# A third chunk made by seven block products in the first net of a two-layer hybrid model, with memory and parameters waiting in the space of the turned memory

## The chip, the cores and the metric

The kernel runs on one core of one Trainium2 chip. The metric is the device time of one execution in microseconds. Engines are named as the profile names them: PE (TensorE, matmul), PEld (its weight loads), DVE (VectorE), ACT (ScalarE), POOL (GpSimd), SP (SyncE, which here only issues transfers).

## What is computed

Two layers. Each runs a gated feed-forward net, a mixer (short convolution, gated linear recurrence, moving averages), cross attention to a memory of 256 rows, and a second net, each followed by a residual with layer norm:

```python
def swiglu(x, w_gate, w_up, w_down):
    return (jax.nn.silu(x @ w_gate) * (x @ w_up)) @ w_down
...
for l in range(DEPTH):
    h = layer_norm(ALPHA * h + 0.5 * swiglu(h, ffn1_gate[l], ffn1_up[l], ffn1_down[l]), ln_g[l, 0], ln_b[l, 0])
    ...
    h = layer_norm(ALPHA * h + cross_attn(h, mem, ca_q[l], ca_k[l], ca_v[l], ca_o[l]), ln_g[l, 2], ln_b[l, 2])
    h = layer_norm(ALPHA * h + 0.5 * swiglu(h, ffn2_gate[l], ffn2_up[l], ffn2_down[l]), ln_g[l, 3], ln_b[l, 3])
```

There are 256 tokens (two blocks of 128), the model's width is 1024, the width inside a net 2816. All is float32.

## The kernel before, in words

**Splitting.** Every float32 factor is split into a high part, rounded to the PE's float32 format by an ACT copy, and a low part, the rest, by a DVE subtraction (`split`, L60 to L62). A product is three matmuls: high by high, high by low, low by high (`mm_rows`, L129). So each weight tile that a transfer brings (`raw`, 128 partitions by 1024 numbers, 512 KB) costs one ACT copy (`whi`, L61) and one DVE subtraction (`wlo`, L62) before PE can use it. There are six raw tiles, eight high and eight low ones; each waits for its last reader before it is filled again.

**A net** (`ffn`, L400) goes through the inner width in chunks of 512: c = 0 to 4, and a last one, 5, of 256. For a chunk, `hidden` (L538) makes gate and up of both token blocks: 8 weight tiles, 96 matmuls. The turned activations then meet the rows of `down`: after chunk c come `both(c - 2, 1)` and `both(c - 1, 0)` (L696), 24 matmuls and two weight tiles each (after chunk 1 only the second of them, and for chunk 5 other ends).

`by_seven` (L568) makes the same chunk from the 2x2 block product (halves of the depth by token blocks; gate and up are the two columns) with seven block products in place of eight: 84 matmuls. For it, sums of blocks of x are made once (`blocks_of_x`, L552: four `quarters` on DVE at L556, four sums at L564, four splits). Of the weights, four blocks of two tiles are loaded: w00 (gate, upper half), w01 (up, upper), w11 (up, lower) and w10 (gate, lower). PE multiplies by w00, w00 + w01, that + w11, w01 + w11, w11, w10 and the last sum + w10, in this order in PE's program (L624 to L638). The sums are made in place by DVE (L597, eight tiles), and all seven are split (14 tiles). Results are put together by DVE (`put`, L619, seven times) and go through the activation in `left` (L641).

w00 is loaded into `spare0` and `spare1`, w01 into the tiles of the layer norm's scale and shift (`lng`, `lnb`), w11 into two raw tiles, w10 into `spare2` and a raw tile (L588 to L591). In the first net the quarters lie in `lng` and `lnb` too (L685).

Which chunks are made by seven is said at L679: 2 and 4 in three of the four nets, only 4 in the first one (`early` is given there).

**The first net's side work.** The small parameters are read into `spare2` and turned by PE (`small_parameters`, L221). The memory is read by 32 transfers on POOL's queue into `spare0` and `spare1` and later turned by DVE and split into `mT` (`load_memory`, L183). Both are begun behind chunk 1's loads (L729). The memory is turned inside chunk 2 (`aside`, L704), the parameters after it (L731). `keys` (L755), the stage after the first net, is the first reader of `mT`.

**Order.** Each engine's instructions are put in a fixed order when the program is built, by a scheduler that lets loads and splits move ahead as far as their tiles are free; on the chip each engine then takes them in that order, and waits at the first one that isn't ready. `tc.issue_after(ins)` adds an order to `ins` for those instructions of its block that run on the same engine as `ins`, and no wait across engines.

Of the kernel before, what the change touches and what calls it, by code (L numbers as in the profile page):

```python
# [17 lines left out]
P = 128  # L18
# [11 lines left out]
LEVELS = (1, 2, 4, 8, 16, 32, 64)  # L30
WINDOWS = (2, 4, 8, 16)
PAD = 16


class Weights:
# [11 lines left out]
def model(ctx: ExitStack, tc: tile.TileContext, t: dict, out: bass.AP):  # L47
# [112 lines left out]
    )  # L160

    xT = cst.tile([P, NK, 2, SEQ], F32R, name="xT")
    mT = cst.tile([P, NK, 2, SEQ], F32R, name="mT")
    xTh, xTl = xT[:, :, 0, :], xT[:, :, 1, :]
    mTh, mTl = mT[:, :, 0, :], mT[:, :, 1, :]
    kTh = cst.tile([P, NK, SEQ], F32R, name="kTh")
    kTl = cst.tile([P, NK, SEQ], F32R, name="kTl")

# [13 lines left out]

    def load_memory(mp, behind):  # L183
        m = [
            mp.tile([P, DM], F32, tag=f"spare{n}", name="m", bufs=1).rearrange("p (k b j) -> p k b j", k=4, j=32)
            for n in range(2)
        ]
        with tc.issue_after(behind.ins):
            for n in range(2):
                for a in range(4):  # L190
                    for k in range(4):
                        c = (4 * n + k) * P + a * 32
                        nc.gpsimd.dma_start(
                            m[n][a * 32 : a * 32 + 32, k],
                            t["mem"][0, :, c : c + 32].rearrange("(b i) j -> i b j", i=32),
                        )

        def later():
            for n in range(2):
                for k in range(0, 4, 2):  # L200
                    turned = mp.tile([P, 2, SEQ], F32, tag="up", name="turned")
                    nc.vector.transpose(
                        turned.rearrange("p k t -> p (k t)"), m[n][:, k : k + 2].rearrange("p k b j -> p (k b j)")
                    )
                    d = slice(4 * n + k, 4 * n + k + 2)
                    split(mTh[:, d, :], mTl[:, d, :], turned)

        return later

# [9 lines left out]
    psc = prm[:, 28:32].rearrange("p (l j) -> p l j", l=DEPTH)  # L219

    def small_parameters(op):  # L221
        spare = op.tile([P, DM], F32, tag="spare2", name="rows", bufs=1)
        rows = spare[:, 0:P]
        nc.gpsimd.memset(rows, 0.0)
        nc.gpsimd.dma_start(rows[0:12, :], t["conv_w"].rearrange("l k (j p) -> (l k j) p", p=P))
        nc.gpsimd.dma_start(rows[12:20, :], t["rec_lb"].rearrange("l (h p) -> (l h) p", p=P))
        nc.gpsimd.dma_start(rows[20:28, :], t["rec_norm_g"].rearrange("l (h p) -> (l h) p", p=P))
        nc.gpsimd.dma_start(rows[28:32, :], t["pool_scale"].rearrange("l (j p) -> (l j) p", p=P))
        nc.gpsimd.memset(wpool, 0.0)
        for g in range(2):  # L230
# [24 lines left out]

        cnt = op.tile([P, 2, PAD], F32, name="cnt", bufs=1)
        wcol = op.tile([P, 2], F32, name="wcol", bufs=1)
        for g, w in enumerate(WINDOWS):
            nc.gpsimd.memset(wcol[(g % 2) * 64 : (g % 2) * 64 + 64, g // 2 : g // 2 + 1], float(w))
        nc.gpsimd.iota(  # L260
            cnt, pattern=[[0, 2], [1, PAD]], base=1, channel_multiplier=0,
            allow_small_or_imprecise_dtypes=True,
        )

        def later():
            pt = acc((P, P))
            nc.tensor.transpose(pt, rows, idn)
            nc.vector.tensor_copy(prm, pt[:, 0:32])
            for j in range(2):
                nc.vector.tensor_scalar_min(cnt[:, j, :], cnt[:, j, :], wcol[:, j : j + 1])  # L270
            nc.vector.reciprocal(invc, cnt)

            lb = [prm[:, 12:16], prm[:, 16:20]]
            mx = op.tile([P, HEADS], F32, name="mx", bufs=1)
            nc.vector.tensor_tensor(mx, lb[0], lb[1], op=ALU.max)
            e = op.tile([P, DEPTH, HEADS], F32, name="e", bufs=1)
            s = op.tile([P, HEADS], F32, name="s", bufs=1)
            for l in range(DEPTH):
                nc.vector.tensor_tensor(e[:, l, :], lb[l], mx, op=ALU.subtract)
            nc.scalar.activation(e, e, AF.Exp)  # L280
# [119 lines left out]
    def ffn(l, name, n, pend=None, last=False, early=None):  # L400
        gate, up, down = (t[f"{name}_{x}"][l] for x in ("gate", "up", "down"))
        with tc.tile_pool(name="ffn", bufs=2, reuse_waits="tile") as fp:
# [273 lines left out]
                return w, ah[:, 2 * u : 2 * u + 2, :], al[:, 2 * u : 2 * u + 2, :]  # L676


            sevens = (2, 4) if early is None else (4,)  # L679
            bx = []  # L680

            if early is None:
# [21 lines left out]
            def aside():  # L704

                with tc.issue_after(lows[-1].ins):
                    if bx:
                        rest[1]()
                    else:
                        bx.extend(blocks_of_x())  # L710

            for c, (c0, ncol) in enumerate(chunks):
                if not c:
                    acts.append(first())
                    ys = [[acc((P, 512), "dn") for _ in range(2)] for _ in range(NT)]
                elif c in sevens:
                    left = by_seven(c0, bx)
                else:
                    if c in (1, 2) and early is not None:
                        acts.append(hidden(c0, aside))  # L720
                    else:
                        acts.append(hidden(c0) if ncol == CHUNK else last_hidden(c0))
                if c == 1 and early is None:
                    bx.extend(blocks_of_x())
                if c == max(sevens) + 1:
                    gb = ln_params(l, n)
                if c == 1 and early is not None:

                    with tc.issue_after(loads[-1].ins):  # L729
                        rest = early(fp)  # L730
                if c == 2 and early is not None:  # L731
                    with tc.issue_after(lows[-1].ins):
                        rest[0]()
                if c > 0:
                    if c > 1:
                        both(c - 2, 1)
                    if c in sevens:
                        acts.append(left())
                    if c < len(chunks) - 1:
                        both(c - 1, 0)  # L740
# [24 lines left out]
    def values(l, c, vh, vl, between={}):  # L765
        w = load(t["ca_v"][l], 0, NK, c * CHUNK, CHUNK)
        for i in range(NT):
            o = acc((P, 512))
            for k in range(NK):
                if k % 2 == 0:  # L770
                    between.get(4 * i + k // 2, lambda: None)()
                wh, wl = w.at(k, slice(0, CHUNK))
                mm_rows(o, mTh[:, k, tok(i)], mTl[:, k, tok(i)], wh, wl, k == 0, k == NK - 1)
            d = slice(c * CHUNK, (c + 1) * CHUNK)
            split(halves(vh[:, i, d]), halves(vl[:, i, d]), sums(o))

# [404 lines left out]


    def beginnings(op):
        parameters, made = small_parameters(op)
        return parameters, load_memory(op, made)

    pend = None
    for l in range(DEPTH):
# [32 lines left out]
```

## Time and profile before

| | |
|---|---|
| three runs | 1070.62, 1070.91, 1071.72 us; median 1070.91 |
| span of the profiled execution, first to last instruction | 1068.8 us; its own time is not listed apart, and the median of the runs is 2.1 us above its span |
| PE busy | 1059.3 us, 99% |
| DVE busy | 946.3 us, 89% |
| ACT busy | 642.4 us, 60% |
| POOL busy | 66.4 us, 6% |
| granted PE clock, mean | 0.998 |
| moved by DMA | 231.90 MB, mean 217 GB/s |
| first net on PE | from 7.64 us on; chunk 2 begins at 54.44, chunk 4 at 116.71 |

Busy times are of one execution. A matmul row's mean duration is longer than the pace at which matmuls follow each other, since they are pipelined; the pace is read from stretches of the chain that ended last (length by count). In the same way a DVE operation's duration overlaps a little with the next one's, so costs of DVE work are read from start to start.

### The profile page before, as it was taken

The page shows a single profiled execution, that of the slowest core. Times are in us where ns is not written, and L with a number is a line of the kernel's source. Part 1 is how long each engine was busy: PE and PEld are TensorE (multiplying, and loading weights), DVE is VectorE, ACT ScalarE, POOL GpSimd, SP SyncE. Part 2 cuts the span into 40 slices and gives each one's busy share as a digit, 9 for nine tenths or more (in the row PEclk, how much of TensorE's full clock was granted, in tenths as well). Part 3 has the DMA queues.
Part 4 walks back from the last instruction along what each step waited for, and adds up shares of the span by engine and source line. Part 5 has one row for each costly group of instructions (what it writes and reads, how often), then busy time and mean ns, then how long its engine had stood idle before and what let it go on. Part 6 is the DMA issues. An engine that isn't in the chain of part 4 may idle for free.

```text
span 1068.8 us, 16312 instructions
## 1 busy us (share of the span) xinstructions
PE 1059.3 (99%) x5966; PEld 937.7 (88%) x5966; DVE 946.3 (89%) x1318; ACT 642.4 (60%) x916; POOL 66.4 (6%) x114
## 2 busy tenths in 40 slices
PE   9999999999999999999999999999999999999997
PEld 7888888889899888888888888888898998888886
DVE  6977997998988799999799999788989787999996
ACT  7555664666557565656575557566764665656660
POOL 9700001000000000000000000010000000000000
PEclk9999999999999999999999999999999999999999
DMA  9997484755574575848675865856536665759461
GB/s 362 262 307 256 129 288 165 249 176 174 170 278 167 178 252 194 290 167 218 238 272 184 256 254 183 290 179 216 196 126 213 241 227 181 257 156 334 134 223 40
DMA packets 130895, 231.90 MB, mean 217 GB/s; under 512 B 9408, under 2 KB 48608, under 8 KB 130816
## 3 DMA queue, kind: packets, MB, share of 16 engines
q1 hardware_dynamic: 129024, 228.49, 64.8%
q0 software_dynamic: 1216, 1.20, 0.5%
q8 instruction: 47, 0.77, 0.3%
q10 hardware_dynamic: 576, 1.18, 0.3%
q14 instruction: 32, 0.26, 0.1%
HBM read 216.15 MB, written 1.05 MB: 203 GB/s over the span
## 4 chain that ended last, share of the span: by engine, by line
PE 99%; DMA 0%; DVE 0%; issue 0%; DVEq 0%
PE acc L105 65%; PE dn L105 31%; PE acc L172 1%; PE dn L923 1%; PE dn L982 0%; DMA h<-in_x_dram 0%; PE acc L491 0%; PE dn L981 0%; PE dn L971 0%; PE acc L1047 0%; PE dn L888 0%; DVE h L358 0%; DVE h L353 0%; PE dn L472 0%; DVE st L338 0%
## 5 line engine op out<-in xcount | busy, mean ns | idle before, releaser
L61 ACT CAST whi<-raw 128x1024 fp32r<-128x1024 f32 (+1 forms) x438 | 442.9, 1042 | 197.5 <-DVE raw L597 54.9
L62 DVE TENSOR_TENSOR wlo<-raw,whi 128x1024 fp32r<-128x1024 f32 (+1 forms) x438 | 515.7, 1209 | 32.6 <-ACT whi L61 29.0
L105 PE MATMUL acc<-whi,xT 128*128 128x512 f32 x1032 | 312.9, 380 | 0.0
L105 PEld LDWEIGHTS acc<-whi,xT 128*128 128x128 f32 x1032 | 195.1, 189 | 27.5
L105 PE MATMUL acc<-wlo,xT 128*128 128x512 f32 x516 | 195.6, 379 | 0.0
L105 PE MATMUL acc<-xT,whi 128*128 128x512 f32 x576 | 142.3, 383 | 0.2
L105 PE MATMUL dn<-whi,ah 128*128 128x512 f32 x346 | 131.5, 380 | 0.0
L105 PE MATMUL dn<-wlo,ah 128*128 128x512 f32 x346 | 131.2, 379 | 0.0
L105 PE MATMUL dn<-whi,al 128*128 128x512 f32 x346 | 131.2, 379 | 0.0
L105 PEld LDWEIGHTS acc<-xT,whi 128*128 128x128 f32 x576 | 104.0, 190 | 12.5 <-ACT whi L61 0.7
L105 PEld LDWEIGHTS acc<-wlo,xT 128*128 128x128 f32 x516 | 97.5, 189 | 13.8
L105 PE MATMUL dn<-whi,xT 128*128 128x512 f32 x288 | 87.9, 381 | 0.0
L105 PEld LDWEIGHTS acc<-xT,wlo 128*128 128x128 f32 x576 | 75.5, 191 | 3.9
L105 PE MATMUL acc<-xT,wlo 128*128 128x256 f32 x576 | 75.9, 275 | 0.0
L105 PEld LDWEIGHTS dn<-whi,al 128*128 128x128 f32 x346 | 65.4, 189 | 9.2
L105 PEld LDWEIGHTS dn<-wlo,ah 128*128 128x128 f32 x346 | 65.4, 189 | 9.2
L105 PEld LDWEIGHTS dn<-whi,ah 128*128 128x128 f32 x346 | 65.4, 189 | 9.1
L350 POOL TENSOR_TENSOR rs<-rs,nhalf 128x1 f32<-128x1 f32 x16 | 14.9, 930 | 833.6 <-DVE rs L346 598.1
L597 DVE TENSOR_TENSOR raw<-raw 128x1024 f32<-128x1024 f32 x56 | 66.2, 1217 | 0.4
L105 PEld LDWEIGHTS dn<-whi,xT 128*128 128x128 f32 x288 | 54.4, 189 | 7.7 <-DVE xT L62 0.3
L105 PE MATMUL dn<-wlo,xT 128*128 128x512 f32 x144 | 54.6, 379 | 0.0
L332 DVE SCALAR_TENSOR_TENSOR h<-h,dn 128x512 f32<-128x512 f32 x31 | 21.2, 683 | 32.9 <-PE dn L105 32.9
(234 smaller groups left out, 1277.5 us busy)
## 6 DMA issues: line engine op xcount, KB each, us to landing
raw<-in_ffn_up_dram SPq DMA_DIRECT2D x88, 512.0 KB, 5.3
raw<-in_ffn_down_dram SPq DMA_DIRECT2D x88, 512.0 KB, 6.6
raw<-in_ffn_gate_dram SPq DMA_DIRECT2D x84, 512.0 KB, 5.1
raw<-in_w_in_dram SPq DMA_DIRECT2D x48, 512.0 KB, 4.7
dealt<-sg SPq DMA_DIRECT2D x80, 128.0 KB, 4.7
raw<-in_ca_k_dram SPq DMA_DIRECT2D x16, 512.0 KB, 4.9
raw<-in_w_out_dram SPq DMA_DIRECT2D x16, 512.0 KB, 4.5
raw<-in_ca_v_dram SPq DMA_DIRECT2D x16, 512.0 KB, 5.3
```

Of the source, the lines that this page charges most:

```text
L61: nc.scalar.copy(hi, src)
L62: lows.append(nc.vector.tensor_tensor(lo, src, hi.bitcast(F32), op=ALU.subtract))
L105: nc.tensor.matmul(o, w, x, start=start, stop=stop)
L172: nc.tensor.transpose(pt[:, k, :], src[:, (4 * j + k) * P : (4 * j + k + 1) * P], unit)
L332: nc.vector.scalar_tensor_tensor(v, v, ALPHA / scale, sums(y[i][n]), op0=ALU.mult, op1=ALU.add, accum_out=None if junk is None else st[:, ...
L350: nc.gpsimd.tensor_tensor(rs, rs, nhalf[:, 0:1], op=ALU.pow)
L597: nc.vector.tensor_tensor(r[i], r[i], plus[i], op=ALU.add)
L923: nc.tensor.matmul(o[g, hh, :], kc[:, hh, g], x, start=True, stop=True)
```

## The change

The first net, too, makes chunk 2 by seven. For that `spare0` to `spare2` must be free at chunk 2. So the parameters' rows and the memory get the space in which the turned memory will lie: two tiles, `mT0` (first rows, then the first half of the turned memory) and `mT1` (first the memory as it was read, then the second half). A small class, `Halves`, makes the two look like one. The parameters are turned after chunk 3's products are written down (c == 3), the memory after chunk 5's (c == 5), and the call that loads the memory stands at c == 3.

```diff
+class Halves:
+    def __init__(self):
+        self.tiles = [None, None]
+    def __getitem__(self, at):
+        k = at[1]
+        if isinstance(k, slice):
+            n = k.start // 4
+            return self.tiles[n][(at[0], slice(k.start - 4 * n, k.stop - 4 * n), *at[2:])]
+        return self.tiles[k // 4][(at[0], k % 4, *at[2:])]
...
-    mT = cst.tile([P, NK, 2, SEQ], F32R, name="mT")
+    mT = Halves()
+    early_rows, early_memory = (cst.tile([P, 2048], F32, tag=f"mT{n}", name=f"early{n}") for n in range(2))
...
     def load_memory(mp, behind):
         m = [
-            mp.tile([P, DM], F32, tag=f"spare{n}", name="m", bufs=1).rearrange("p (k b j) -> p k b j", k=4, j=32)
-            for n in range(2)
+            early_memory[:, n * DM : (n + 1) * DM].rearrange("p (k b j) -> p k b j", k=4, j=32) for n in range(2)
         ]
...
         def later():
             for n in range(2):
-                for k in range(0, 4, 2):
-                    turned = mp.tile([P, 2, SEQ], F32, tag="up", name="turned")
+                turned = [mp.tile([P, 2, SEQ], F32, tag="up", name="turned") for _ in range(2)]
+                for k in range(2):
                     nc.vector.transpose(
...
+                mT.tiles[n] = cst.tile([P, 4, 2, SEQ], F32R, tag=f"mT{n}", name=f"mT{n}")
+                for k in range(2):
+                    d = slice(4 * n + 2 * k, 4 * n + 2 * k + 2)
+                    split(mT[:, d, 0, :], mT[:, d, 1, :], turned[k])
...
     def small_parameters(op):
-        spare = op.tile([P, DM], F32, tag="spare2", name="rows", bufs=1)
+        spare = early_rows[:, 0:DM]
...
-            sevens = (2, 4) if early is None else (4,)
+            sevens = (2, 4)
...
                 with tc.issue_after(lows[-1].ins):
-                    if bx:
-                        rest[1]()
-                    else:
-                        bx.extend(blocks_of_x())
+                    bx.extend(blocks_of_x())
...
-                    if c in (1, 2) and early is not None:
+                    if c == 1 and early is not None:
                         acts.append(hidden(c0, aside))
...
-                if c == 2 and early is not None:
+                if c == 3 and early is not None:
                     with tc.issue_after(lows[-1].ins):
                         rest[0]()
+                    turn_memory = load_memory(fp, loads[-1])
+                if c == 5 and early is not None:
+                    with tc.issue_after(lows[-1].ins):
+                        turn_memory()
...
     def beginnings(op):
-        parameters, made = small_parameters(op)
-        return parameters, load_memory(op, made)
+        return small_parameters(op)
```

`keys` and `values` read `mT` through `Halves` and are otherwise as before. In the changed kernel the line numbers from `split` on are 14 to 17 higher; the texts below use those of the kernel before, and say so where they don't.

More of the change, by code (lines that the diff above doesn't have):

```diff
@@ L162, in model @@
     xT = cst.tile([P, NK, 2, SEQ], F32R, name="xT")
-    mT = cst.tile([P, NK, 2, SEQ], F32R, name="mT")
+    mT = Halves()
     xTh, xTl = xT[:, :, 0, :], xT[:, :, 1, :]
-    mTh, mTl = mT[:, :, 0, :], mT[:, :, 1, :]
+    early_rows, early_memory = (cst.tile([P, 2048], F32, tag=f"mT{n}", name=f"early{n}") for n in range(2))
     kTh = cst.tile([P, NK, SEQ], F32R, name="kTh")
@@ L199, in later @@
             for n in range(2):
-                for k in range(0, 4, 2):
-                    turned = mp.tile([P, 2, SEQ], F32, tag="up", name="turned")
+                turned = [mp.tile([P, 2, SEQ], F32, tag="up", name="turned") for _ in range(2)]
+                for k in range(2):
                     nc.vector.transpose(
-                        turned.rearrange("p k t -> p (k t)"), m[n][:, k : k + 2].rearrange("p k b j -> p (k b j)")
-                    )
-                    d = slice(4 * n + k, 4 * n + k + 2)
-                    split(mTh[:, d, :], mTl[:, d, :], turned)
+                        turned[k].rearrange("p k t -> p (k t)"),
+                        m[n][:, 2 * k : 2 * k + 2].rearrange("p k b j -> p (k b j)"),
+                    )
+                mT.tiles[n] = cst.tile([P, 4, 2, SEQ], F32R, tag=f"mT{n}", name=f"mT{n}")
+                for k in range(2):
+                    d = slice(4 * n + 2 * k, 4 * n + 2 * k + 2)
+                    split(mT[:, d, 0, :], mT[:, d, 1, :], turned[k])
         return later
@@ L772, in values @@
                 wh, wl = w.at(k, slice(0, CHUNK))
-                mm_rows(o, mTh[:, k, tok(i)], mTl[:, k, tok(i)], wh, wl, k == 0, k == NK - 1)
+                mm_rows(o, mT[:, k, 0, tok(i)], mT[:, k, 1, tok(i)], wh, wl, k == 0, k == NK - 1)
             d = slice(c * CHUNK, (c + 1) * CHUNK)
```

## The prediction

> **What bounds the kernel now.** I read the page's busy shares first, then the chain that ended last.
>
> ```profile
> PE 1059.3 (99%) x5966; PEld 937.7 (88%) x5966; DVE 946.3 (89%) x1318; ACT 642.4 (60%) x916; POOL 66.4 (6%) x114
> ```
>
> PE is at work for all but 9.5 us of the span, so fewer matmuls shorten it, as long as nothing else becomes late. Next the chain in order of time (start, length, what): chunk 2 of the first net (96 matmuls), chunk 4 by seven (84), and chunk 2 of the second net by seven.
>
> ```profile
> 54.44 20.72 PE acc L105 x96
> ...
> 116.71 18.13 PE acc L105 x84
> ...
> 415.80 18.13 PE acc L105 x84
> ```
>
> A matmul costs 20.72/96 = 0.216 us, and chunk 2 by seven saves **20.72 - 18.13 = 2.59 us**: the whole gain there is. The question is whether DVE, at 89%, keeps up. The timeline of DVE around chunk 4 gives its prices; an operation's cost is taken from its start to the next one's.
>
> ```profile
> 109.40 3.49 DVE L597 TENSOR_TENSOR raw<-raw 128x1024 f32<-128x1024 f32 x3
> 112.81 2.35 DVE L62 TENSOR_TENSOR wlo<-raw,whi 128x1024 fp32r<-128x1024 f32 x2
> 115.08 2.36 DVE L597 TENSOR_TENSOR raw<-raw 128x1024 f32<-128x1024 f32 x2
> 117.35 1.30 DVE L453 STREAM_TRANSPOSE square<-dealt 128x512 f32<-128x512 f32 x2
> 118.57 1.19 DVE L62 TENSOR_TENSOR wlo<-raw,whi 128x1024 fp32r<-128x1024 f32 x1
> 119.67 1.28 DVE L62 TENSOR_TENSOR al<-square,ah 128x512 fp32r<-128x512 f32 x2
> 120.88 5.76 DVE L62 TENSOR_TENSOR wlo<-raw,whi 128x1024 fp32r<-128x1024 f32 x5
> 126.55 0.69 DVE L619 TENSOR_TENSOR half<-acc,sg 128x512 f32<-128x512 f32 x1
> 127.15 2.35 DVE L62 TENSOR_TENSOR wlo<-raw,whi 128x1024 fp32r<-128x1024 f32 x2
> ```
>
> A low part costs 5.67/5 = 1.134 us, a sum of weights 3.41/3 = 1.137, two transposes 1.22, two low parts of activations 1.21, a `put` 0.60. Chunk 4's fourteenth low part is ready at 127.15 + 2.35 = 129.5. PE has 78 of the 84 matmuls ahead of its use: 116.71 + 78 x 0.216 = 133.5. So chunk 4 is fed with 4.0 us to spare.
>
> **Chunk 2, DVE's ledger.** DVE's instruction order in the changed kernel (built, not run) is fixed. From the first quarter of x to chunk 2's fourteenth low part it holds 4 quarters, 20 low parts of weights, 8 sums of weights, 4 sums of quarters, 4 low parts of these, 8 `gated`, 4 transposes, 4 low parts of activations, 4 `put`. DVE's rows before, from the quarters on:
>
> ```profile
> 23.74 2.48 DVE L62 TENSOR_TENSOR wlo<-raw,whi 128x1024 fp32r<-128x1024 f32 x2 [2.22 <-ACT whi L61]
> 26.14 2.85 DVE L556 TENSOR_TENSOR quarters<-xT 128x512 f32<-128x512 f32 x4
> 28.91 1.21 DVE L62 TENSOR_TENSOR wlo<-raw,whi 128x1024 fp32r<-128x1024 f32 x1
> 30.05 0.68 DVE L564 TENSOR_TENSOR quarters<-quarters 128x512 f32<-128x512 f32 x1
> 30.65 1.21 DVE L62 TENSOR_TENSOR wlo<-raw,whi 128x1024 fp32r<-128x1024 f32 x1
> 31.78 0.74 DVE L440 TENSOR_TENSOR sg<-acc,sg 128x256 f32<-128x256 f32 x2
> 32.45 0.68 DVE L62 TENSOR_TENSOR kTl<-quarters,kTh 128x512 fp32r<-128x512 f32 x1
> ```
>
> Four quarters 2.77, a sum of quarters 0.60, a low part of them (as long by its row) 0.60, two `gated` 0.67. The ledger: 2.77 + 20 x 1.134 + 8 x 1.137 + 8 x 0.60 + 4 x 0.67 + 2 x 1.22 + 2 x 1.21 + 4 x 0.60 = **49.3 us**. Started at 26.14 and never idle, DVE ends it at 75.4. PE wants that part at 54.44 + 78 x 0.216 = 71.3. So even with no wait at all DVE is 4.1 us late. Chunk 4 had its spare time from a DVE that ran ahead of PE; here chunk 2 follows chunk 1 by 24 matmuls only, and DVE has no idle time to draw on between 26.14 and 43.00 (first row of this table by windows: stretch, its length, then busy time of PE, PEld, DVE, ACT, POOL, granted clock, DMA share, GB/s):
>
> ```profile
> 26.14:43.00 16.86, 16.86 (x80) 14.77 (x79) 16.86 (x25) 8.77 (x13) 15.42 (x27) 1.00 0.98 257
> 5.00:25.00 20.00, 20.00 (x98) 17.17 (x97) 16.13 (x20) 17.33 (x26) 19.55 (x33) 1.00 1.05 402
> ```
>
> **The start of the ledger moves.** In SP's new order w00 (two loads) and the first half of w10 stand ahead of the end of chunk 0's up, because the spare tiles are free from the start. They are 3 x 512 KB = 1.57 MB, and the DMA was full at 402 GB/s from 5 to 25 us: 3.9 us for all loads behind them. ACT's rows:
>
> ```profile
> 17.94 1.06 ACT L61 CAST whi<-raw 128x1024 fp32r<-128x1024 f32 x1 [0.36 <-DMA raw<-in_ffn_gate_dram]
> 19.21 1.05 ACT L61 CAST whi<-raw 128x1024 fp32r<-128x1024 f32 x1 [0.21 <-DMA raw<-in_ffn_gate_dram]
> 20.27 1.28 ACT L436 ACT_TABLE_LOAD   x1
> 21.57 1.21 ACT L436 ACTIVATE sg<-dn 128x256 f32<-128x256 f32 x4
> 22.64 4.02 ACT L61 CAST whi<-raw 128x1024 fp32r<-128x1024 f32 x4
> ```
>
> Chunk 1's first copy comes at 17.94 + 3.9 = 21.8. The changed order then has the activations (20.27 to 22.64, 2.4 us) and after them the other three copies at 1.0 each: the fourth ends at 28.3 and its low part at 29.6, where the quarters began at 26.14 before. Chunk 0's and 1's weights still come in time (the last tile of chunk 0's up is split by 22.5; PE wants it 12 + 96 + 24 matmuls ahead of 54.44, at 25.9), but the ledger starts **3.5 us later** and ends at 78.9. PE is then 78.9 - 71.3 = **7.6 us** late at the end of chunk 2. Bounds: 4.1 if the early loads cost nothing; 1 to 3 us more if w01 comes late, for it may be loaded only when the quarters are read. By the ledger DVE has read those in `lnb` at 43, and the sum that needs w01 is due at 51; for the load of `raw` issued at 43.1 before, the answer is
>
> ```profile
> DMA to landing us min/median/max: 9.2/9.2/9.2
> ```
>
> 9.2 us, but then it stood behind others that now are issued later or are gone ahead. I take 7.6: a queue that was full delays what is put behind.
>
> [...]
>
> **The rest, at nothing.** *Chunk 3*: from chunk 2's last low part to chunk 4's first one DVE has 17 low parts, five operations of 0.6 and a turn of 2.4, 24.7 us; PE has 192 matmuls, 41.4 us. DVE is ahead again, and would stay so with 16 us more. *Chunk 4* gets the parameters' small operations, before here:
>
> ```profile
> 89.93 0.18 DVE L268 COPY prm<-acc 128x32 f32<-128x32 f32 x1
> ...
> 94.14 2.36 DVE L62 TENSOR_TENSOR wlo<-raw,whi 128x1024 fp32r<-128x1024 f32 x2
> ```
>
> 4.21 us with two low parts inside, so 1.9 of their own; three `put` more (1.8) now stand ahead of the last part. Spare time: 4.0 - 1.9 - 1.8 = 0.3, so nothing, or up to 1 us if a wait falls in. *Memory turned at the end*: four transposes and four low parts (2.44 + 2.42 us) go where DVE waits for PE:
>
> ```profile
> 164.78 0.69 DVE L332 SCALAR_TENSOR_TENSOR h<-h,dn 128x512 f32<-128x512 f32 x1 [1.55 <-PE dn L105]
> ...
> 168.67 0.69 DVE L332 SCALAR_TENSOR_TENSOR h<-h,dn 128x512 f32<-128x512 f32 x1 [3.19 <-PE dn L105]
> ```
>
> 1.55 + 3.19 = 4.74 hide it nearly; without that cover it is 2 us, since `keys` and the layer norm wait behind it. *Memory loads* don't move: the call's order is tied to a load on SP, the transfers are on POOL, and in POOL's new order they stand where they stood, the first two a few instructions earlier. Their row before, 32 KB each:
>
> ```profile
> 27.79 9.24 POOL L193 DMA_DIRECT2D m<-in_mem_dram  x16
> ```
>
> They crowd the DMA from 28 us on as before, beside the loads on which the ledger hangs. That is the part of the change that doesn't do what it says; did they move to chunk 3, the sum would lose only the term for a late w01, so the forecast stays. *Parameters in `mT0`* cost nothing: same operations, POOL has no other work there.
>
> **The sum**, against the profiled span: 1068.8 - 2.6 + 7.6 = 1073.8; the median of the runs lies 2.1 above the span, so **1075.9, say 1076.0 us**.
>
> **Rivals.**
> *Clock.* PE would wait some 3.6 us in one piece before the seventh product (by the ledger the twelfth part is ready at 72.6, so the sixth product ends at 73.9 or 74; the thirteenth part is ready at 77.7). At the end of the program, after the last matmul, the granted clock (last but two in the second row) fell:
>
> ```profile
> 1061.22 0.28 PE L105 MATMUL acc<-whi,al 128*128 128x256 f32 x1
> ```
>
> ```profile
> 1064.00:1064.50 0.50, 0.00 (x0) 0.00 (x0) 0.50 (x2) 0.00 (x0) 0.00 (x0) 0.52 0.00 0
> ```
>
> So 2.5 us of idling, 1061.5 to 1064, can halve it. If it stays so for as long as the wait, PE loses half of 3.6: 1.8, time 1077.8. [...] For it: the row; against it: there the idling had no end, while here the waits come in pieces with products between them.
> *Early loads free.* Late by 4.1 only: 1070.9 - 2.6 + 4.1 = 1072.4. For it: the ledger's start hangs on ACT as well, which was waiting only 0.2 to 0.4 us for each load; against it: 402 GB/s with nothing left over.
> *DVE in time* (not slower): as in the other nets, where two chunks by seven pass without a wait (415.80 above). It takes DVE reaching the last part by 71.3, 7.6 us earlier than the ledger; from 73.9 on the gain is gone. Then 1070.9 - 2.6 = 1068.3. For it: three nets; against it: there DVE enters chunk 2 further ahead (its transposes inside that chunk start 6.1 us after PE's start, at 421.86, here about 13 us after).
>
> ```profile
> 421.86 1.30 DVE L453 STREAM_TRANSPOSE square<-dealt 128x512 f32<-128x512 f32 x2
> ```
>
> *More goes wrong* (w01 late, chunk 4 short as well): about 1079.5.
>
> **Chances.** Forecast 0.48, clock 0.22, early loads free 0.14, in time 0.12, more 0.04. 0.2% is 2.1 us (about what a measurement can tell): faster below 1068.8, slower above 1073.0. The first two and the last are slower, and 0.03 of the early loads': **0.77**; the rest of these, 0.11, is the same; 0.12 faster. The range leaves out the case in time and part of the last: **1071.8 to 1079.5**.
>
> **What would show it.** Right: in chunk 2 PE waits for DVE's `wlo` and ACT's `whi`, about 7 to 8 us in all, most before the last two products; DVE is without idle from 30 to 79 us; the quarters start near 29.6; chunk 3 and later have no waits; the first net ends 5 us later. Wrong: quarters at 26 (early loads free), a clock under 1 near 78 us, PE busy through chunk 2, waits in chunk 4 or before `keys`.

## The result and the profile after

Before: 1070.91 us (five executions, 1070.62 to 1071.72). After: **1078.76 us** (five, 1076.98 to 1081.36). The ratio is 1.0074, with a 95% interval of 1.0062 to 1.0086: slower, by 7.85 us between the medians. Line numbers below are those of the changed kernel: L76 is the low part (L62 before), L613 the sum of weights (L597), L635 `put` (L619), L572 the quarters (L556), L348 to L374 the layer norm (L332 to L358), L215 the turning of the memory (L202).

The profiled execution is the fastest of the five: 1076.98 us, span 1075.3, 6.5 more than the span before. First its busy shares, beside those of before (PE 1059.3, DVE 946.3):

```profile
PE 1060.5 (99%) x5954; PEld 936.9 (87%) x5954; DVE 964.2 (90%) x1337; ACT 648.2 (60%) x921; POOL 62.9 (6%) x114
```

PE has 12 instructions fewer and isn't busy for a shorter time: part of it ran at half the clock (3.4 us in chunk 2, shown below). DVE has 18 us more. Next what PE waited for (engine and tile, the releaser; us in total, times, the longest):

```profile
PE acc L119 <- DVE wlo L76: 2.3, 2, 1.6
PE acc L119 <- DVE half L635: 2.1, 1, 2.1
PE dn L488 <- DVE kTh L483: 1.5, 1, 1.5
PE acc L186 <- DVE h L374: 0.8, 1, 0.8
PE acc L507 <- DMA h<-in_x_dram: 0.5, 1, 0.5
```

The third and fifth are at the start of the program, in both kernels. The first two are chunk 2's, the fourth is new too. Where they are shows in the chain that ended last (start, length, what), here from the end of chunk 2 to `keys`:

```profile
77.80 2.64 PE acc L119 x11
80.45 10.36 PE dn L119 x48
90.81 20.72 PE acc L119 x96
...
122.00 18.13 PE acc L119 x84
...
183.75 7.86 PE acc L119 x48
```

Chunk 4 (84 matmuls) starts at 122.00, where it was 116.71: 5.29 later, so 5.29 + 2.59 = **7.9 us** were lost up to there. Of these, 7.3 are chunk 2's own: from its first matmul (54.88) to the first one behind it (80.28) are 25.4 us in place of 18.1. The other 0.6 are a later arrival of PE at chunk 2 (its first matmul started at 54.28 before). `keys` starts at 183.75. Its row before is:

```profile
177.28 7.86 PE acc L105 x48
```

6.47 later, so another 1.2 is lost behind chunk 4. From there on nothing changes: -2.6 + 7.9 + 1.2 = 6.5, the difference of the spans.

DVE's timeline in chunk 2, from its first quarter to the fourteenth low part:

```profile
29.85 2.49 DVE L572 TENSOR_TENSOR quarters<-xT 128x512 f32<-128x512 f32 x4
...
67.21 1.29 DVE L469 STREAM_TRANSPOSE square<-dealt 128x512 f32<-128x512 f32 x2
...
70.74 0.68 DVE L635 TENSOR_TENSOR half<-acc,sg 128x512 f32<-128x512 f32 x1
...
76.54 4.62 DVE L76 TENSOR_TENSOR wlo<-raw,whi 128x1024 fp32r<-128x1024 f32 x4
```

The quarters start 3.7 us later than before (26.14). DVE is never idle between them and 90.97. The last row's first two parts are the thirteenth, ready at 76.54 + 1.13 = 77.7, and the fourteenth, at 78.8; PE goes on at 77.80. PE's three larger waits are these:

```profile
62.80 0.48 PE L119 MATMUL acc<-wlo,kTh 128*128 128x512 f32 x1 [0.71 <-DVE wlo L76]
...
71.47 0.48 PE L119 MATMUL acc<-whi,xT 128*128 128x512 f32 x1 [2.14 <-DVE half L635]
...
77.80 0.48 PE L119 MATMUL acc<-wlo,xT 128*128 128x512 f32 x1 [1.57 <-DVE wlo L76]
```

The first is for a low part of the third product. The second is not for a missing low part: the matmul's own inputs, `whi` and `xT`, are not made by a `put`, so what the sixth product waits for is an accumulator (`acc`, a tile in which PE adds up a product) that the first `put` (70.74) reads and so sets free. That `put` stands behind two transposes, a low part of weights and two of activations in DVE's order. The third wait is for the thirteenth low part. Between the last two, the windows of 1 us show the clock (PE busy, PEld, DVE, ACT, POOL; the granted clock; DMA share, GB/s):

```profile
72.00:73.00 1.00, 1.00 (x5) 0.85 (x4) 1.00 (x2) 0.00 (x0) 0.00 (x0) 0.78 0.67 258
73.00:74.00 1.00, 1.00 (x3) 0.76 (x3) 1.00 (x2) 0.20 (x1) 0.00 (x0) 0.50 0.00 0
74.00:75.00 1.00, 1.00 (x4) 0.79 (x3) 1.00 (x2) 0.84 (x1) 0.00 (x0) 0.50 0.00 0
75.00:76.00 1.00, 1.00 (x4) 0.56 (x2) 1.00 (x3) 0.47 (x1) 0.00 (x0) 0.51 0.00 0
76.00:77.00 1.00, 0.23 (x1) 0.00 (x0) 1.00 (x3) 1.00 (x2) 0.00 (x0) 1.00 0.53 66
```

The clock halved after the 2.14 us wait, for (0.22 + 0.50 + 0.50 + 0.49) / 0.5 = 3.4 us, and the sixth product took 4.3 us (71.47 to 75.73) in place of 2.6. But PE had done it, and the one matmul of the seventh that was ready, by 76.2, and then had to wait 1.6 us for the low part in any case. Here the half clock cost nothing; it only turned waiting into slow work. So of chunk 2's 7.3 us the three waits are 4.4 and the half clock 1.7; the rest are a short wait at 60.5 (0.25), the last matmul ahead of each wait (0.38 by its row, where the pace is 0.216) and the first one behind it, which is slower than the others (0.32 to the next start).

The 1.2 us behind chunk 4 stand at the first token block's layer norm. DVE's rows:

```profile
168.63 1.29 DVE L215 STREAM_TRANSPOSE turned<-early 128x512 f32<-128x512 f32 x2
...
172.15 1.29 DVE L215 STREAM_TRANSPOSE turned<-early 128x512 f32<-128x512 f32 x2
173.37 0.65 DVE L348 SCALAR_TENSOR_TENSOR h<-h,dn 128x512 f32<-128x512 f32 x1
...
174.13 1.29 DVE L76 TENSOR_TENSOR mT<-turned,mT 128x512 fp32r<-128x512 f32 x2
175.34 0.68 DVE L348 SCALAR_TENSOR_TENSOR h<-h,dn 128x512 f32<-128x512 f32 x1
```

Before, the two additions to `h` (L332) started 48.07 and 51.96 us after chunk 4's start (164.78 and 168.67 less 116.71), each right when PE had its sum ready. Now they start 51.37 and 53.34 after it: DVE is still at the memory, and in its order the low parts of the second turning (174.13) stand between the two additions. The second is 1.4 later, PE then waits 0.8 for `h`, and takes the eight turns of `h` in two lots (1.29 us, where it was 0.87): 1.2.

### The profile page after: what moved, and what is told of

The parts are those of the page before. It is cut to its first block, busy times and chain, and to the rows that moved or that the text cites. A ratio compares the mean times of both kernels' runs of the same rounds, so it can differ in the third digit from the quotient of the medians.

```text
span 1075.3 us, 16291 instructions
## 1 busy us (share of the span) xinstructions
PE 1060.5 (99%) x5954; PEld 936.9 (87%) x5954; DVE 964.2 (90%) x1337; ACT 648.2 (60%) x921; POOL 62.9 (6%) x114
## 4 chain that ended last, share of the span: by engine, by line
PE 92%; DVE 5%; DMA 1%; issue 1%; ACT 1%; DVEq 0%; ACTq 0%
PE acc L119 60%; PE dn L119 29%; DVE wlo L76 2%; PE acc L186 1%; DMA raw<-in_ffn_gate_dram 1%; DVE raw L613 1%; PE dn L940 1%; ACT whi L75 0%; PE dn L999 0%; DMA h<-in_x_dram 0%; DVE sg L456 0%; PE acc L507 0%; DVE square L469 0%; DVE quarters L572 0%; DVE quarters L580 0%
## 5 line engine op out<-in xcount | busy, mean ns | idle before, releaser
L75 ACT CAST whi<-raw 128x1024 fp32r<-128x1024 f32 (+1 forms) x444 | 447.8, 1041 | 209.6 <-DVE raw L613 71.0
L76 DVE TENSOR_TENSOR wlo<-raw,whi 128x1024 fp32r<-128x1024 f32 (+1 forms) x444 | 521.5, 1207 | 33.7 <-ACT whi L75 30.4
L119 PE MATMUL acc<-whi,xT 128*128 128x512 f32 x992 | 302.5, 381 | 2.1 <-DVE half L635 2.1
L119 PEld LDWEIGHTS acc<-whi,xT 128*128 128x128 f32 x992 | 188.2, 190 | 29.3 <-DVE half L635 2.5
L119 PE MATMUL acc<-wlo,xT 128*128 128x512 f32 x496 | 188.7, 381 | 1.6 <-DVE wlo L76 1.6
L119 PEld LDWEIGHTS acc<-wlo,xT 128*128 128x128 f32 x496 | 94.0, 190 | 15.5 <-DVE wlo L76 2.2
L613 DVE TENSOR_TENSOR raw<-raw 128x1024 f32<-128x1024 f32 x64 | 75.6, 1214 | 0.3
L119 PE MATMUL acc<-wlo,kTh 128*128 128x512 f32 x128 | 48.7, 381 | 0.8 <-DVE wlo L76 0.7
```

The costliest lines, as they stand in the source:

```text
L75: nc.scalar.copy(hi, src)
L76: lows.append(nc.vector.tensor_tensor(lo, src, hi.bitcast(F32), op=ALU.subtract))
L119: nc.tensor.matmul(o, w, x, start=start, stop=stop)
L613: nc.vector.tensor_tensor(r[i], r[i], plus[i], op=ALU.add)
```

## The experiments

**Theory**: DVE's work from the quarters to chunk 2's fourteenth low part is longer than PE's, and starts late because of chunk 2's early loads; PE waits for it. **Rivals**: the half clock; the early loads cost nothing; the moved memory and parameters cost the time; the blocks' landing. All times in us:

| kernel | median (lowest to highest) | ratio to before, 95% |
|---|---|---|
| changed, again | 1077.71 (1077.22 to 1078.52) | 1.0049 to 1.0077 |
| changed, third time | 1078.59 (1077.30 to 1078.65) | 1.0055 to 1.0080 |
| only the moves | 1071.31 (1070.86 to 1073.13) | 0.9997 to 1.0015 |
| without chunk 2's sums | 1068.75 (1068.20 to 1069.33) | 0.9969 to 0.9987 |
| late block loads | 1076.55 (1075.72 to 1078.12) | 1.0041 to 1.0066 |
| late memory loads | 1077.17 (1076.55 to 1078.49) | 1.0046 to 1.0072 |
| memory turned in chunk 3 | 1080.17 (1078.78 to 1081.50) | 1.0070 to 1.0098 |
| two products made twice | 1076.14 (1075.96 to 1077.25) | 1.0036 to 1.0061 |
| late block loads, products twice | 1074.59 (1074.14 to 1075.02) | 1.0020 to 1.0044 |
| eight sums on POOL | 1084.40 (1083.28 to 1084.69) | 1.0106 to 1.0137 |
| four sums on POOL | 1081.41 (1080.65 to 1082.31) | 1.0083 to 1.0110 |
| late block loads, four sums on POOL | 1078.20 (1077.26 to 1078.36) | 1.0052 to 1.0077 |

The fifteen executions of the changed kernel have a median of 1078.52. The program's order of DVE's work is made anew when an edit changes the program; where that matters it is said.

**Only the moves.** The change without its seven products.

```diff
-            sevens = (2, 4)
+            sevens = (2, 4) if early is None else (4,)
...
-                    if c == 1 and early is not None:
-                        acts.append(hidden(c0, aside))
+                    if c in (1, 2) and early is not None:
+                        acts.append(hidden(c0, aside if c == 1 else lambda: None))
```

> The change without its seven products: the first net's chunk 2 is made by eight as before, but memory and parameters wait where the turned memory will lie and are turned and made where the change puts them. Theory (the moves alone cost little, the loss is chunk 2's): 1070.9 to 1072, a wait of up to 0.8 us ahead of the keys, none in chunk 2 to 4. Rival (the moves are what costs): 1073 or more.

1071.31, not to be told from before: as the theory says. Memory and parameters may lie and be turned where the change puts them; the loss is chunk 2's. PE has no wait at the layer norm; in this kernel's order both turnings of the memory stand ahead of the first addition to `h`. The profiled execution, 1073.09, is one of the two slowest: its quarters start only at 33.16, and PE waits 1.6 us behind chunk 1.

**Without chunk 2's sums.** The eight sums of weights are left out; the matmuls and the low parts stay as many.

```diff
-                        if plus is not None:
+                        if plus is not None and not (early is not None and c0 == 2 * CHUNK):
```

> Leaves out the eight sums of weight blocks that DVE makes for the first net's chunk 2 (the products are made with unsummed blocks, so as many matmuls and low parts as before). Theory (DVE's work in chunk 2 is the bound): 8 x 1.137 = 9.1 us less on DVE, the fourteenth low part is ready near 70, PE wants it at 71.3 plus what the early loads cost ahead of chunk 2, so no wait there, or under 1 us; time 1070.9 - 2.6 + 0.8 = 1069.1, 1068.5 to 1070.5. Rival (the clock, or the DMA of the late blocks, holds PE up): a wait of 3 us or more stays in chunk 2 or the matmuls run at half the clock there, time 1074 or more.

1068.75, faster than before by 2.2. Its chain at chunk 2 and the start of chunk 3, and behind them chunk 3's row before:

```profile
54.59 18.13 PE acc L119 x84
72.72 10.36 PE dn L119 x48
83.08 20.72 PE acc L119 x96
```

```profile
85.63 20.72 PE acc L105 x96
```

Chunk 2 by seven runs through in 18.13, and chunk 3 starts at 83.08, where it was 85.63 before and 90.81 in the changed kernel. Yet the quarters start as late as there (29.97, not 29.85). So 9.1 us of DVE's work decide; neither the clock nor the blocks' landing holds PE up when they are gone. The layer norm's wait is gone too; here as well both turnings stand ahead of the first addition to `h`.

**Late block loads.** Chunk 2's blocks are issued behind the loads of chunk 0, chunk 1 and `down`.

```diff
+                with tc.issue_after(loads[-1].ins) if early is not None and c0 == 2 * CHUNK else nullcontext():
-                w00 = block(gate, 0, pieces("spare0", "spare1"))
+                    w00 = block(gate, 0, pieces("spare0", "spare1"))
...
```

> The four block loads of the first net's chunk 2 are issued behind chunk 0's, chunk 1's and down's loads on SP instead of ahead of some of them. Theory (the early loads push DVE's work back by 3.5 us): the quarters start near 26.3 instead of 29.85, the fourteenth low part of chunk 2 is ready near 76 to 76.6 instead of 78.8 (two operations more stand ahead of it in this order), PE waits 4 to 5.5 us in chunk 2 instead of 7.9, and the time falls by 2.5 to 3.5 us against the changed kernel: 1075 to 1076. Rival (the early loads are served beside the others and cost nothing, ACT's order sets the start): quarters near 29 still, time 1078 to 1079. Second rival (the block loads, now late, become the bound themselves): quarters near 26, but DVE idle in chunk 2 with a DMA named, and time 1078 or more.

1076.55: 1.2 under the changed kernel's time in the same series, 2.0 under that of all fifteen; less than expected. The quarters' start, PE's longest wait, and chunk 3's start:

```profile
26.58 2.84 DVE L572 TENSOR_TENSOR quarters<-xT 128x512 f32<-128x512 f32 x4
```

```profile
76.28 0.48 PE L119 MATMUL acc<-whi,xT 128*128 128x512 f32 x1 [2.14 <-ACT whi L75]
```

```profile
88.93 20.72 PE acc L119 x96
```

The 3.3 us at the start come back as expected (26.58, not 29.85), which shows that the early loads cost them. At chunk 3 only 1.9 are left of it: two more of the `put` (72.66 and 73.26) now stand ahead of the last sum of weights, for the seventh product, and ACT can copy that sum only then. Chunk 4 waits 0.4 for a copy as well. What DVE gains at one end its new order spends at the other.

ACT's copies of chunk 0's last two up pieces in the changed kernel show where the early loads stood; behind them the last one's row before:

```profile
17.95 1.06 ACT L75 CAST whi<-raw 128x1024 fp32r<-128x1024 f32 x1 [2.87 <-DMA raw<-in_ffn_up_dram]
20.53 1.04 ACT L75 CAST whi<-raw 128x1024 fp32r<-128x1024 f32 x1 [1.52 <-DMA raw<-in_ffn_up_dram]
```

```profile
16.52 1.05 ACT L61 CAST whi<-raw 128x1024 fp32r<-128x1024 f32 x1 [0.22 <-DMA raw<-in_ffn_up_dram]
```

The last one is copied 4.0 us later, after two new waits for its queue: the price of 1.57 MB at 402 GB/s that the prediction worked out.

**Late memory loads.** A small DVE operation on the memory's space in chunk 4 holds POOL's loads back.

```diff
+                    with tc.issue_after(lows[-1].ins):
+                        nc.vector.memset(early_memory[:, 0:2048:32], 0.0)
                     turn_memory = load_memory(fp, loads[-1])
```

> POOL's loads of the memory wait for one small operation (64 elements in each partition set to zero, 0.2 us) that DVE does in chunk 4, so that the loads really move to where the change says, out of the 28 to 46 us in which chunk 2's blocks are loaded. Theory (DVE's work, not the landing of the blocks, is late in chunk 2): the waits of PE in chunk 2 stay, 7 to 8 us, time 1077 to 1079. Rival (the memory loads crowd the block loads and delay DVE's start, or make the executions uneven): the quarters start before 28.5 us or the blocks land earlier, time 1073 to 1076, runs within 1 us.

POOL's first load and the quarters:

```profile
126.61 5.81 POOL L206 DMA_DIRECT2D early<-in_mem_dram  x10 [104.54 <-DVE e L295]
```

```profile
30.02 2.49 DVE L572 TENSOR_TENSOR quarters<-xT 128x512 f32<-128x512 f32 x4
```

The loads moved by 100 us, and the quarters start no earlier. Chunk 2's larger waits are those of the changed kernel (2.14 and 1.60). The median is 1.4 us under that of the fifteen. In the profile 0.7 of the layer norm's 1.2 are gone: DVE's order differs behind chunk 2, both turnings of the memory now stand ahead of the first addition to `h`, and PE hardly waits there, though it still takes the turns of `h` in two lots. The rest of the 1.4 the profile does not show.

**Memory turned in chunk 3** (and the parameters made one chunk earlier).

```diff
-                if c == 3 and early is not None:
+                if c == 2 and early is not None:
                     with tc.issue_after(lows[-1].ins):
                         rest[0]()
                     turn_memory = load_memory(fp, loads[-1])
-                if c == 5 and early is not None:
-                    with tc.issue_after(lows[-1].ins):
-                        turn_memory()
...
-                    bx.extend(blocks_of_x())
+                    if bx:
+                        turn_memory()
+                    else:
+                        bx.extend(blocks_of_x())
...
-                    if c == 1 and early is not None:
+                    if c in (1, 3) and early is not None:
```

> The turning of the memory on DVE is put inside chunk 3 instead of in front of the layer norm of the first token block, and the parameters' small operations one chunk earlier. Theory (the turning delays that layer norm, and PE waits 0.8 us for it ahead of the keys): that wait goes, time 0.8 us less than the changed kernel, 1077.5 to 1078.3; chunk 2's waits stay at 7 to 8 us. Rival (the wait there has another reason, the order of h and dn): 1078.5 to 1079 as before. Second rival (turned in chunk 3 it makes chunk 4's low parts late): a new wait in chunk 4 of 1 to 3 us, time 1079 to 1081.

The second rival: 1080.17. The wait at the layer norm is gone, and chunk 4 has new ones:

```profile
138.15 0.48 PE L119 MATMUL acc<-whi,xT 128*128 128x512 f32 x1 [0.44 <-ACT whi L75]
139.41 0.48 PE L119 MATMUL acc<-wlo,xT 128*128 128x512 f32 x1 [0.78 <-DVE wlo L76]
141.70 0.48 PE L119 MATMUL acc<-whi,xT 128*128 128x512 f32 x1 [0.94 <-ACT whi L75]
142.65 0.70 PE L119 MATMUL dn<-whi,ah 128*128 128x512 f32 x2 [0.46 <-ACT whi L75]
```

From chunk 3's start to the end of `both` behind chunk 4 PE takes 154.35 - 91.09 = 63.3 us here and 150.49 - 90.81 = 59.7 in the changed kernel: 3.6 us more, for 4.9 us of turning. So DVE has about a microsecond to spare through chunks 3 and 4, no more.

**Two products made twice.**

```diff
-                w10 = block(gate, 1, pieces("spare2", "raw"))
+                w10 = raw10 = block(gate, 1, pieces("spare2", "raw"))
...
-                run(o[0], bx[3], parts_of(w11))
-                run(o[1], part_of_x(0, 1), parts_of(w10))
-                run(o[2], part_of_x(1, 1), parts_of(w00, w10))
+                w11, w10 = parts_of(w11), parts_of(w10)
+                for _ in range(2 if early is not None and c0 == 2 * CHUNK else 1):
+                    run(o[0], bx[3], w11)
+                for _ in range(2 if early is not None and c0 == 2 * CHUNK else 1):
+                    run(o[1], part_of_x(0, 1), w10)
+                run(o[2], part_of_x(1, 1), parts_of(w00, raw10))
```

> In the first net's chunk 2 the fifth and the sixth product are each made twice, the second time from the start over the first, so that PE works (24 matmuls, 5.2 us) where it waits in the changed kernel; DVE's order up to the fourteenth low part is the same. Theory (the end of chunk 2 is set by DVE alone, and the half clock at 72.6 to 76 lies inside the wait): the same time, 1077 to 1078.8, chunk 2's last two products start near 77.8 as before. Rival (the clock, halved after the wait, costs 1 to 2 us in those executions that are slower than the profiled one): granted clock 1.00 throughout chunk 2, and the median falls to 1076.5 to 1077.2 with all runs within 1 us of each other. If 24 more matmuls lengthen the time by 5 us, PE was the bound after all.

24 matmuls more, and 1076.14, below both the theory's and the rival's figure. PE's wait for the thirteenth low part and a window that had half the clock in the changed kernel:

```profile
78.12 0.48 PE L119 MATMUL acc<-wlo,xT 128*128 128x512 f32 x1 [0.49 <-DVE wlo L76]
```

```profile
74.00:75.00 1.00, 1.00 (x6) 0.88 (x5) 1.00 (x2) 0.89 (x1) 0.00 (x0) 1.00 0.00 0
```

The clock stays at 1.00, and PE goes on with the last product at 78.12, with quarters at 30.17 (77.80 and 29.85 in the changed kernel): filling the waits moves the end of chunk 2 not at all, so PE wasn't the bound and the half clock cost nothing there. What this kernel gains in its profile is the layer norm's 1.2: again DVE's order behind chunk 2 changed, with both turnings ahead of `h`. Its median lies further under the changed kernel's, by 2.4, and that rest the profile does not show.

**The changed kernel again, and a third time**, for the spread of its executions.

> The changed kernel once more, for the 2 us by which its other executions exceed the profiled one. If the profiled execution was a fast one by chance, another profile shows 1078 to 1079, and the difference lies in one place: PE waits in chunk 2 of about 10 us instead of 7.9 (clock rival: matmuls at half the clock that no wait covers, 1 to 2 us; DMA rival: a load that lands later and DVE idle in front of it).

> The changed kernel a third time, for one more profile and five more times. If the clock makes the spread, executions with a mean clock of 0.995 lie 2 us or more above those of 0.997, and a profile of 1078.5 or more shows half clock outside the waits; if not, the slower executions have the same clock, and some other row differs.

The second profile (1077.22) shows which engine sets the end of chunk 2. PE came to chunk 2 at 56.43, 1.55 later than in the first; yet the first matmul behind chunk 2 is only 0.22 later (80.50, 80.28), just as the quarters are (30.07, 29.85). So that end goes by DVE's start, not by PE's. The third (1078.59) is 1.6 us longer; its first quarter and the end of chunk 2:

```profile
31.29 2.49 DVE L572 TENSOR_TENSOR quarters<-xT 128x512 f32<-128x512 f32 x4
```

```profile
81.88 10.36 PE dn L119 x48
```

The start is 1.44 later (31.29, 29.85), the end of chunk 2 1.43 (81.88, 80.45), `keys` 1.44 (185.19, 183.75). ACT's first copy for chunk 1 starts at 23.35 in place of 21.91, after 1.68 us of idling in place of 0.34: a later opening is passed on to the end. That a load of `gate` landed later there is the author's reading; the row names PE, which came to chunk 2 at 54.68, no later than in the first. In this series the clock doesn't sort the times: 1078.65 had a mean clock of 0.999, 1077.30 one of 0.997. Only the slowest of the fifteen, 1081.36, stands out with 0.995; it has no profile, and its cause stays open.

**Late block loads with two products made twice**: both edits.

> The late block loads (alone 1076.55) with the fifth and sixth product made twice (alone 1076.14). Theory (DVE's order sets the end of chunk 2, early loads cost 2 us of it, and filling the waits takes away what the clock adds): 1074 to 1075.5, granted clock 1.00 in chunk 2, runs within 1.2 us of each other. Rival (what the doubled products gained has to do with another order of DVE's work, not with the clock): 1076 to 1077. If the 24 matmuls don't fit in the waits any more, 1 to 2 us more than that.

1074.59, the best of the changed kernels that make all their sums, and still 0.3% slower than before. It fits the first theory's figure, but not for its reason: in the profiles chunk 3 starts at 89.85, later than with late loads alone (88.93), since the 24 matmuls are now longer than the waits. The gain is that chunk 4 and the layer norm have no wait any more, by another order of DVE's work.

**Sums on POOL**: all eight, the last four, and the last four with late block loads.

```diff
-                            nc.vector.tensor_tensor(r[i], r[i], plus[i], op=ALU.add)
+                            e = nc.gpsimd if early is not None and c0 == 2 * CHUNK and pool else nc.vector
+                            e.tensor_tensor(r[i], r[i], plus[i], op=ALU.add)
...
-                run(o[3], bx[2], parts_of(w01, w11))
+                run(o[3], bx[2], parts_of(w01, w11, True))
...
-                run(o[2], part_of_x(1, 1), parts_of(w00, w10))
+                run(o[2], part_of_x(1, 1), parts_of(w00, w10, True))
```

`pool` is a third argument of `parts_of`, False where it isn't given; with all eight sums on POOL it is left out.

> All eight sums of weight blocks of the first net's chunk 2 are made on POOL instead of DVE; the rest as in the changed kernel. DVE has then the same work as in the run without sums, whose time was 1068.75. Theory (only DVE's work is the bound): if POOL makes a sum in less than about 2.5 us, the eight are done between 46.5 us (the end of POOL's loads of memory) and 66, in time for the low parts: 1069 to 1070.5. Rival (POOL is too slow or starts too late): DVE and PE wait for POOL in chunk 2, and the time is 1073 or more; with 4 us for a sum the last would end near 79 and its two products after it, so 1080 or more.

> Only the last four of these sums (for the fourth and the seventh product) go to POOL. Theory (DVE's work): 4 x 1.137 = 4.5 us less on DVE, the fourteenth low part near 74.3 instead of 78.8, PE 3 us late in chunk 2 instead of 7.9, time 1072.5 to 1074. Rival (POOL late): a wait for POOL in chunk 2, 1076 or more. The clock rival: with shorter waits no clock under 1 in chunk 2, so the runs lie closer together than the 4.4 us of the changed kernel.

> Both together: chunk 2's block loads issued behind the others (which alone gave 1076.55) and the last four sums on POOL. Theory (the two delays add up): DVE starts 3.3 us earlier and has 4.5 us less, so the fourteenth low part is ready near 71 to 72, PE waits less than 1 us in chunk 2, time 1069 to 1070.5, which would be faster than the kernel before. Rival (late blocks or POOL become the bound): a wait of 2 us or more for ACT's copies or POOL, 1072 or more.

All three times are the rival's: 1084.40, 1081.41, 1078.20. With four sums, POOL's first two and what DVE did beside them:

```profile
51.78 6.43 POOL L614 TENSOR_TENSOR raw<-raw 128x1024 f32<-128x1024 f32 x2 [4.59 <-DMA raw<-in_ffn_gate_dram]
```

```profile
52.74 6.56 DVE L76 TENSOR_TENSOR wlo<-raw,whi 128x1024 fp32r<-128x1024 f32 x2
```

A sum takes POOL 3.2 us, and each low part beside it takes DVE 3.28 instead of 1.13. The low parts beside the other two sums take 3.4 each. So the four sums take 4.5 us off DVE and put some 9 on it. And here the half clock does cost something, for the product behind the wait has nothing more to wait for; the same kernel's chain and a window:

```profile
78.24 7.13 PE acc L119 x24
```

```profile
80.00:81.00 1.00, 1.00 (x4) 0.82 (x3) 1.00 (x3) 1.00 (x2) 0.00 (x0) 0.50 0.42 53
```

24 matmuls in 7.13 us; at full clock it is 24 x 0.216 = 5.18, so 1.95 are lost, of which 3.4 us at half the clock explain 1.7.

## Why the prediction was right, and where it was off

It forecast 1076.0 us, slower, range 1071.8 to 1079.5; measured 1078.76. The mechanism was the one forecast. That the range held the time is in part luck: its upper end had been set for a late w01 and a short chunk 4, neither of which came, and other losses filled that room. Term by term:

- *The gain, 2.59*: right. It comes in full where DVE keeps up (chunk 3 at 83.08 without the sums, 85.63 before).
- *The ledger, 49.3*: right to 0.4. From 29.85 to 78.8 are 49.0.
- *The later start, 3.5, from the early loads*: right, 3.7 in the changed kernel, and 3.3 of it went when they were issued later. That what stands behind those loads waits for the whole of them, 3.9, was the author's estimate, which no row of before showed; the runs showed 4.0 at ACT's last copy of chunk 0's up. That a kernel without them would be 3.5 faster in the end was wrong: 1.2 to 2.0, because DVE's order changes with the loads.
- *PE late by 7.6*: 7.9 measured. The division was not as forecast. PE's waits in chunk 2 are not 7 to 8 us for low and high parts, with a single one of 3.6 before the seventh product's, but 0.7 in the third product, 2.14 at the sixth for an accumulator, then 1.57, and a slow product between. The ledger counted the `put` as work and missed that the first of them holds an accumulator; the sum hardly cares, since PE waits for the ledger's end in any case.
- *The rest, at nothing*: **the step that was mis-sized**. "1.55 + 3.19 = 4.74 hide it nearly" took the cover from a DVE which in the old kernel waited there for PE. In the new one 1.2 us are lost, and a wait before `keys` was one of the signs that the prediction had named for being wrong. The prediction gave 2 us for the case without cover and did not put it into the sum. By the runs it hangs on DVE's order, though none changed that alone: here the second turning's low parts stand between the two additions to `h`. With the two products made twice both turnings stand ahead of the first addition, and the loss is gone, though DVE was as late in chunk 2; with late memory loads, in the same order, it is 0.5. Chunk 4's spare time, 0.3 by the prediction, is 0.4 (its fourteenth low part is ready at 138.4, PE wants it at 122.00 + 78 x 0.216 = 138.85). That DVE would stay ahead "with 16 us more" in chunk 3 was wrong: 4.9 more there cost 3.6. The count stopped at chunk 4's first low part and left out that chunk's own sums and parts.
- *Memory loads don't move, and it wouldn't matter*: both right (POOL's loads stand at 21 to 46.5 us; held back to 126.61 they free nothing in chunk 2).
- *From span to median, 2.1*: mis-sized. The profiled execution is 1.7 above its span, but the median of its five is another 1.8 above that. With chunk 2 by seven, as the third profile shows, a late start of DVE is handed on in full; with chunk 2 by eight it seems to be partly hidden behind PE (only the moves: quarters at 33.16, and 1.8 above the median). That the executions without a profile were late for the same reason is not shown. So the 2.76 between forecast and median are 0.3 (PE late), 1.2 (layer norm) and 1.4 (from span to median), less 0.1 of rounding.
- *Clock rival*: the clock did halve, as the rival had it from the end of the program, after 2.14 us of waiting; it stayed so for 3.4 us, where the rival took the wait's 3.6. It cost nothing in chunk 2, for the wait comes again behind it; the two products made twice show that. Its time, 1077.8, is nearer to the median than the forecast's, by luck.
- *DVE in time*, *early loads free*: against the trace; the first came true only without the sums (1068.75, by the prediction 1068.3).

Open: the 1081.36 execution, why the kernels with two products made twice spread less, and a version with the saved matmuls and without DVE's loss. None of the kernels that make all their sums beats the one before.

## What to carry to other kernels

Before an engine is given work so that another does less, add up the ledger of the first one between two fixed points of that stage, not over the program: here 49 us of work stood against 45 us of time in a kernel that on average had 11% to spare. An idle stretch in the old profile is cover only if the engine will still arrive early at it; after a change that makes that engine late, price the step without its cover. And loads that a new tile lets go early can delay what is behind them on their queue (here by 4.0 us, for 1.57 MB), while every edit may let the scheduler reorder the rest, so compare the end of each stage and not one wait.

## What the runs showed of the hardware

- The granted clock halved after a wait of PE of 2.14 us in four profiles (the changed kernel's three, and that with late memory loads), each time for 3.4 us; in the changed kernel's first profile from 72.56 to 75.97. It halved as well at waits of 2.46 us (both kernels with four sums on POOL) and of 2.55 us (eight sums). It did not, in the windows up to 84 us, at a wait of 2.14 us with late block loads, nor at waits of 2.14 and 2.43 us with the memory turned in chunk 3. So the length of one wait doesn't tell. Behind the last matmul it fell after 2.5 us in the kernel before (1061.50 to 1064.02) and after 4.7 us in the changed one (1067.99 to 1072.66). By the windows, the full clock between two halvings lasted 10.2 us with eight and with four sums on POOL, 6.8 us with late block loads and four sums, and 996.69 us in the changed kernel (75.97 to 1072.66): 3, 3, 2 and 292 times the 3.41 us of a half stretch. So it may be the place of a wait that decides; that was not shown.
- With four sums on POOL, DVE's low parts, which have two inputs, took 3.28 us each beside sums of 3.2, and 1.13 without. With all eight sums there, DVE's `gated` products, of whose two inputs one is an accumulator, kept their pace beside a sum (four in 1.40 us, 1.41 before).
